# Second block's attention: probabilities as the stationary operand of the values matmul

## The chip, the cores and the metric

One core of a Trainium2 chip runs the whole program. The metric is the time of one execution on the device, in microseconds (us); the median of several runs counts. The engines are PE (matrix multiply, with PEld for its weight loads), DVE (vector), ACT (scalar), POOL and SP (which issues transfers).

## What is computed

Two transformer blocks on one sequence of 512 tokens of width 1024, in fp32. The first has a sliding-window and a differential attention and a convolutional feed-forward part. The second block, in which the change lies, has an attention over the 128 keys or so that an index picks for each query, beside a recurrent branch:

```python
logits = jnp.einsum('bthc,btkc->bthk', ql.astype(f32), c_sel)      # 16 heads
logits = logits - slopes[None, None, :, None] * dist[:, :, None, :]
logits = jnp.where(valid[:, :, None, :], logits, -jnp.inf)
p = jax.nn.softmax(logits, axis=-1)
o = jnp.einsum('bthk,btkc->bthc', p, c_sel)
...
y_attn = (o * jax.nn.silu(g_attn)) @ w_attn_proj
```

## The kernel before

Activations are held transposed: eight tiles of 128 features by 512 tokens. Every projection is a "unit" of 128 output features: 8 steps over the input features, each three matmuls with 512 moving columns (high and low parts of weights and activations, `mm3`), accumulated in a PSUM bank. Weights come in by DMA and are split into high and low parts by ACT and by DVE or POOL, some units ahead.

The order of issue isn't written out. The projection loop emits a step and then calls `sched`, which lets generators (`spawn`) go on where a small cost model (`account`) says that their engine and inputs are ready; a generator yields a hint ("T" for PE, "D" for DVE, "A" for ACT) ahead of its next operation. `account` prices each operation and keeps a clock for each engine. The prices set the order only; on the chip each engine takes its instructions in that order and waits for semaphores. All instructions go through one helper, so the trace puts nearly all of them on line 214.

The stage of the change is the loop at the end of `block2` that runs, for each of 8 pairs of heads t, the unit `q{t}` (queries) and the unit `ga{t}` (gate), and then the units `ma0` to `ma2`; behind it the loop waits until all eight results `ao` are there and goes on with the units `wa0` to `wa7`. When the queries and keys of a pair are there, a queue (one item every 2.5 us at most) starts `mla(t, b)` for the four blocks b of 128 queries, in the order 3, 2, 1, 0. Block b sees n = (b + 1) x 128 keys. One `mla`:

- logits of two heads (e = 0, 1) into two banks of the tag "lg" (two banks in all);
- on DVE, for each head, mask and distance added and the minimum taken, into `Lm`;
- on ACT, for each head, the exponential in place, with its row sums into `l`;
- on DVE the reciprocal of the two sums, and for each head `Lm` scaled by it (lines 1741 to 1744);
- for each head b + 1 transposes of 128x128 on PE into a bank of the tag "pt" (two banks), copied by ACT into `PTm`: keys on the partitions, queries along the columns;
- the values matmuls: for each key block c and head e, the values `V` (128 keys by 64) are loaded as the stationary operand and `PTm` (128 keys by 128 queries) moves through, into the 64 partitions of head e of the bank `po` (tag "o"). The output is features by queries, as the rest of the block wants it.

After the four blocks of a pair the gate `g` is multiplied with `po`, and the product is split into high and low parts `ao`. In the first block `swa` and `diff` do the same step with the probabilities loaded and the values moving; `swa` loads 64 columns of queries at a time, `diff` 128, with 128 columns of values moving.

In the names of the trace, `ps_o<-PTm,V` is a matmul that moves `PTm` over the loaded `V` into `po`, `ps_o<-vtok,PTd` is `diff`'s and `ps_o<-va,PT` is `swa`'s. An fp32 matmul shows as two records of load and matmul, one of the transposes or of the projections as one.

Of the kernel before, what the change touches and what calls it, by code (L numbers as in the profile page):

```python
# [15 lines left out]
OP = mybir.AluOpType  # L16

P = 128
S = 512
D = 1024  # L20
# [213 lines left out]
class _Build:  # L234
# [53 lines left out]
    def account(self, key, op, args, kw):  # L288
        aps = [a for a in list(args) + list(kw.values()) if isinstance(a, bass.AP)]
        outs = [a for n, a in kw.items() if n in ("out", "accum_out") and isinstance(a, bass.AP)]  # L290
        if "out" not in kw:
            outs.append(args[0])
        oid = set(id(a) for a in outs)
        n = max(a.free_size() if callable(a.free_size) else a.free_size for a in aps)
        t = self.free[key]
        t00 = t
        for a in aps:
            nm, r = self.region(a)
            f = self.wf.get(nm)
            if f and not (key == "T" and id(a) in oid):  # L300
                t = max([t] + [f.get(i, 0.0) for i in r])
            if id(a) in oid:
                f = self.rf.get(nm)
                if f:
                    t = max([t] + [f.get(i, 0.0) for i in r])
        if key == "T":
            n = outs[0].free_size() if callable(outs[0].free_size) else outs[0].free_size
            m = args[1].free_size() if callable(args[1].free_size) else args[1].free_size
            if op == "transpose":
                c = 0.109  # L310
            elif args[1].dtype == F32R:
                c = max(n / 2400.0, 0.1) + 0.003
            elif m <= 64:
                c = max(n / 930.0, 0.08)
            else:
                c = max(4 * n / 2400.0, 0.21) + 0.004
        elif key == "D":
            c = 0.07 + n * 0.00104
            if op == "tensor_copy" and not any(a.name.startswith("ps_") for a in aps):
                c = 0.07 + n * 0.00052  # L320
            if op in ("tensor_tensor_scan", "scalar_tensor_tensor"):
                c += 0.06
            elif op == "tensor_scalar" and not any(a.name.startswith("ps_") for a in aps):
                c = 0.13 + n * 0.00052
        elif key == "A":
            c = 0.094 + n * 0.000833
            if any(a.name.startswith("ps_") for a in aps):
                c -= 0.042
            c += n * 0.000182 * sum(isinstance(kw.get(x), bass.AP) for x in ("scale", "bias"))
            if "accum_out" in kw:  # L330
                c += 0.093
            if op == "activation":
                f = args[2] if len(args) > 2 else kw["func"]
                if f == AF.Tanh:
                    f = self.fam if self.fam is not None and self.fam != 3 else 0
                else:
                    f = FAM.get(f)
                if f is not None and f != self.fam:
                    self.fam = f
                    c += 1.28  # L340
        elif key == "P":
            c = 0.15 + n * 0.0021
        else:
            c = n * P * 4 / 350000.0
        e = t + c
        self.free[key] = e
        for a in aps:
            nm, r = self.region(a)
            f = (self.wf if id(a) in oid else self.rf).setdefault(nm, {})
            for i in r:  # L350
                f[i] = max(f.get(i, 0.0), e + LAT[key])
        if key != "S":
            self.fin = max(self.fin, e + LAT[key])
        self.last = (t, e)
        self.issued += 1
# [980 lines left out]
    def block2(self, nx):  # L1336
        nc, T = self.nc, self.T
        xs, rb = nx["xs"], nx["rb"]
        wuk, wuv, wrg, wrt = [], [], [], []
        for n in range(4):  # L1340
            t = self.slot("wrg")
            nc.scalar.dma_start(t, self.ins["wrg"][:, n, :])
            wrt.append(t)
        for n in range(2):
            t = self.slot("wuv")
# [341 lines left out]
        for n in range(2):  # L1687
            t = self.slot("wuk")
# [31 lines left out]
        def mla(t, b):  # L1720
            d = pair[t]
            n = (b + 1) * P
            m, l, Ls, xt = self.sm("m2", 2), self.sm("l2", 2), [], []
            yield "T"
            pls = yield from self.psw("lg", 2)
            self.logits(pls, d["q"], d["k"], b, 0, n)
            for e in range(2):
                yield "D"
                L = self.slot("Lm")
                nc.vector.tensor_tensor_reduce(out=L[:, :n], in0=Dt[b][:, :n], in1=pls[e][:, :n], op0=OP.add,  # L1730
                                               op1=OP.min, scale=SLOPES2[2 * t + e], scalar=3e38,
                                               accum_out=m[:, e:e + 1])
                self.rel(pls[e])
                Ls.append(L)
            pls = None
            for e in range(2):
                yield "A"
                nc.scalar.activation(Ls[e][:, :n], Ls[e][:, :n], AF.Exp, bias=m[:, e:e + 1], scale=-1.0,
                                     accum_out=l[:, e:e + 1])
            yield "D"  # L1740
            rr = self.sm("r2", 2)
            nc.vector.reciprocal(rr, l)
            for e in range(2):
                nc.vector.tensor_scalar(Ls[e][:, :n], Ls[e][:, :n], rr[:, e:e + 1], None, op0=OP.mult)
            for e in range(2):
                yield "T"
                pt = yield from self.psw("pt")
                for c in range(b + 1):
                    nc.tensor.transpose(pt[:, c * P:(c + 1) * P], Ls[e][:, c * P:(c + 1) * P], self.ident)
                x = self.slot("PTm")  # L1750
                yield "A"
                nc.scalar.activation(x[:, :n], pt[:, :n], AF.Copy)
                self.rel(pt)
                xt.append(x)
            Ls = None
            yield "T"
            while d["po"] is None and self.psn["o"] > 1:
                yield "T"
            if d["po"] is None:
                d["po"] = self.ps("o")  # L1760
            po = d["po"]
            for c in range(b + 1):
                for e in range(2):
                    hc = (2 * t + e) * 64
                    vt = V[c][hc // 512]
                    nc.tensor.matmul(po[64 * e:64 * e + 64, b * P:(b + 1) * P], vt[:, hc % 512:hc % 512 + 64],
                                     xt[e][:, c * P:(c + 1) * P], start=(c == 0), stop=(c == b))
            xt = None
            d["n"] += 1
            if d["n"] < 4:  # L1770
                return
            while f"ga{t}" not in T:
                yield
            yield "D"
            g = T.pop(f"ga{t}")
            nc.vector.tensor_mul(g, g, d["po"])
            self.rel(d["po"])
            self.dump(f"ao{t}", g)
            del pair[t]
            yield "A"  # L1780
            ao[t] = yield from self.split(g, None, name="ao")
# [3 lines left out]
        for t in range(8):  # L1785
            self.unit(f"q{t}", xs2, ev_q(t))
            qm["items"] += [(lambda t=t, b=b: t in pair and b in Dt and "V" in cell, mla(t, b))
                            for b in (3, 2, 1, 0)]
            self.unit(f"ga{t}", xs2, ev_act(f"ga{t}", AF.Silu))
# [154 lines left out]
```

## Time and profile before

| what | value |
|---|---|
| median of 3 runs | 1333.4 us (1333.04 to 1334.54) |
| the profiled execution's own time | 1329.96 us |
| its span, first to last instruction | 1328.1 us |
| PE busy | 1290.4 us, 97% |
| PE weight loads busy | 1065.6 us, 80% |
| DVE busy | 901.3 us, 68% |
| ACT busy | 708.0 us, 53% |
| POOL busy | 301.8 us, 23% |
| mean granted TensorE clock | 0.99 |

The durations below are from the one profiled execution, the time of the kernel from separate runs. A matmul's record lasts longer than its share of the engine, since matmuls are pipelined; what one costs is read from start to start.

### The profile page before, as it was taken

Reading aid. Unit: us, or ns where it says so; the run is one execution under the profiler, and the core shown is the slowest. Engines: PE = TensorE matmul, PEld = TensorE weight load, DVE = VectorE, ACT = ScalarE, POOL = GpSimd, SP = SyncE. Lnnn points to the kernel's source line nnn. Section 1 sums busy time; section 2 is a strip of 40 time slices with the busy share of each in tenths; the row PEclk is TensorE's granted clock in tenths of the full one; section 3 lists DMA queues with packets and bytes.
Section 4 is the critical chain, followed back from the end, with each engine's and each line's share of the span. In section 5 each row is a group of like instructions: output and inputs, shape, how many; then the busy total and the mean of one; then the engine's idle time right before and its main releaser. Section 6 shows DMA issues by size and latency. Waiting matters only on the chain.

```text
span 1328.1 us, 17863 instructions
## 1 busy us (share of the span) xinstructions
PE 1290.4 (97%) x6748; PEld 1065.6 (80%) x6748; DVE 901.3 (68%) x1586; ACT 708.0 (53%) x1258; POOL 301.8 (23%) x204
## 2 busy tenths in 40 slices
PE   9999998999999999999999988999999999999997
PEld 7788888888888888888887875888788778787886
DVE  6768768776266736674677689588989676753354
ACT  7598765344234313432344455888771778783332
POOL 4301015223034303330333353031220000010111
PEclk9999999999999999999999989999999999999998
DMA  6302240233323332333224410222223121122321
GB/s 234 89 24 64 65 146 30 64 95 96 109 81 95 95 111 80 95 95 107 85 95 132 138 48 16 64 80 79 80 94 114 64 64 48 49 63 96 95 65 64
DMA packets 34245, 113.23 MB, mean 85 GB/s; under 512 B 3824, under 2 KB 5872, under 8 KB 34160
## 3 DMA queue, kind: packets, MB, share of 16 engines
q1 hardware_dynamic: 32192, 109.48, 26.4%
q10 hardware_dynamic: 1968, 2.62, 0.6%
q8 instruction: 53, 0.87, 0.3%
q14 instruction: 32, 0.26, 0.1%
HBM read 109.99 MB, written 2.10 MB: 84 GB/s over the span
## 4 chain that ended last, share of the span: by engine, by line
PE 76%; DVE 16%; ACT 4%; issue 2%; DMA 1%; SPq 0%; POOL 0%; ACTq 0%; DVEq 0%; POOLq 0%
PE ps_mm L214 58%; PE ps_lg L214 8%; PE ps_o L214 8%; DVE c L214 3%; PE ps_pt L214 3%; DVE sq L214 1%; DVE xl L214 1%; DVE sl L214 1%; DVE score L214 1%; ACT wh L214 1%; ACT c L214 1%; DVE wl L214 1%; DVE yo L214 1%; DVE m L214 1%; ACT L214 1%
## 5 line engine op out<-in xcount | busy, mean ns | idle before, releaser
L214 PE MATMUL ps_mm<-xh,wh 128*128 128x512 f32 x840 | 336.8, 401 | 0.0
L214 PE MATMUL ps_mm<-xh,wl 128*128 128x512 f32 x840 | 331.1, 394 | 0.1
L214 PE MATMUL ps_mm<-xl,wh 128*128 128x512 f32 x840 | 330.8, 394 | 0.0
L214 POOL TENSOR_TENSOR wl<-wr,wh 128x1024 fp32r<-128x1024 f32 (+1 forms) x69 | 166.4, 2412 | 423.5 <-ACT wh L214 423.5
L214 ACT ACTIVATE wh<-wr 128x1024 fp32r<-128x1024 f32 (+1 forms) x179 | 185.4, 1038 | 130.9 <-PE ps_mm L214 96.8
L214 DVE SCALAR_TENSOR_TENSOR c<-u,vec,c 128x511 f32<-128x511 f32 (+1 forms) x128 | 171.6, 1342 | 74.8 <-ACT c L214 72.5
L214 PEld LDWEIGHTS ps_mm<-xh,wl 128*128 128x128 f32 x840 | 158.5, 189 | 38.7 <-POOL wl L214 0.8
L214 PEld LDWEIGHTS ps_mm<-xh,wh 128*128 128x128 f32 x840 | 158.7, 189 | 36.5 <-issue 2.0
L214 PEld LDWEIGHTS ps_mm<-xl,wh 128*128 128x128 f32 x840 | 158.8, 189 | 33.6 <-DVE xl L214 0.2
L214 DVE TENSOR_TENSOR wl<-wr,wh 128x1024 fp32r<-128x1024 f32 (+1 forms) x110 | 134.3, 1221 | 72.5 <-ACT wh L214 72.1
L214 ACT ACT_TABLE_LOAD x65 | 83.4, 1283 | 6.0 <-PE ps_mm L214 2.5
L214 PE MATMUL ps_mm<-acth,wh 128*128 128x512 f32 x216 | 84.3, 390 | 2.3 <-DVE fs L214 2.3
L214 PE MATMUL ps_mm<-actl,wh 128*128 128x512 f32 x216 | 84.1, 389 | 0.0
L214 PE MATMUL ps_mm<-acth,wl 128*128 128x512 f32 x216 | 84.1, 389 | 0.0
L214 ACT ACTIVATE acth<-c 128x512 fp32r<-128x512 f32 x32 | 20.2, 632 | 114.0 <-DVE c L214 111.2
L214 ACT ACTIVATE c<-c 128x512 f32<-128x512 f32 x32 | 20.2, 632 | 81.8 <-DVE c L214 81.8
L214 ACT ACTIVATE c<-u,vec 128x512 f32<-128x512 f32 x64 | 51.5, 808 | 13.5 <-DVE u L214 13.5
L214 POOL TENSOR_TENSOR sq<-sq,sq 128x256 f32<-128x256 f32 (+1 forms) x38 | 36.1, 950 | 92.4 <-ACT sq L214 77.9
L214 DVE TENSOR_TENSOR u<-ps_mm,rbn 128x512 f32<-128x512 f32 (+1 forms) x63 | 42.5, 676 | 15.1 <-PE ps_mm L214 15.1
L214 PEld LDWEIGHTS ps_mm<-acth,wh 128*128 128x128 f32 x216 | 40.5, 188 | 11.8 <-DVE fs L214 2.7
L214 POOL MEMSET skl<- 64x512 f32 x28 | 14.7, 526 | 147.4 <-PE ps_pt L214 62.7
L214 PEld LDWEIGHTS ps_mm<-actl,wh 128*128 128x128 f32 x216 | 40.5, 188 | 8.4
(407 smaller groups left out, 2640.9 us busy)
## 6 DMA issues: line engine op xcount, KB each, us to landing
wr<-in_wpk_dram SPq DMA_DIRECT2D x197, 512.0 KB, 3.6
xres<-in_xt_dram SPq DMA_DIRECT2D x8, 256.0 KB, 5.5
wr<-in_wpk_dram SPq DMA_DIRECT2D x6, 256.0 KB, 5.6
wrg<-in_wrg_dram ACTq DMA_DIRECT2D x4, 256.0 KB, 4.2
out_dram<-o SPq DMA_DIRECT2D x4, 256.0 KB, 2.2
out_dram<-o ACTq DMA_DIRECT2D x3, 256.0 KB, 2.2
con<-in_con_dram SPq DMA_DIRECT2D x1, 576.0 KB, 6.1
wuv<-in_wukv_dram ACTq DMA_DIRECT2D x2, 256.0 KB, 5.4
```

Source lines behind the costliest of these rows:

```text
L214: r = f(*a, **k)
```

## The change

In `mla` the two scalings by the reciprocal sums go; the sums of all four blocks are kept in one tile of eight columns per pair (`l8`). The values matmul has its operands exchanged: `PTm` (128 keys by 128 queries) is loaded, and the 64 columns of `V` move. The output `po` is now queries by features, 64 columns for each block and head. After the fourth block, one reciprocal of the eight sums, one product of `po` with them (broadcast over 64 columns) into `y`, four transposes of `y` on PE into a bank of the tag "pt", and the gate is multiplied with that bank. `po` is given back after the product, where before it was given back after the gate. In the cost model, the price of such a matmul falls out of a floor that is changed from 0.21 to 0.115 us; with 128 moving columns the price stays as it was.

```diff
             else:
-                c = max(4 * n / 2400.0, 0.21) + 0.004
+                c = max(4 * n / 2400.0, 0.115) + 0.004
...
-            m, l, Ls, xt = self.sm("m2", 2), self.sm("l2", 2), [], []
+            m, Ls, xt = self.sm("m2", 2), [], []
+            if "l" not in d:
+                d["l"] = self.sm("l8", 8)
...
                 nc.scalar.activation(Ls[e][:, :n], Ls[e][:, :n], AF.Exp, bias=m[:, e:e + 1], scale=-1.0,
-                                     accum_out=l[:, e:e + 1])
-            yield "D"
-            rr = self.sm("r2", 2)
-            nc.vector.reciprocal(rr, l)
-            for e in range(2):
-                nc.vector.tensor_scalar(Ls[e][:, :n], Ls[e][:, :n], rr[:, e:e + 1], None, op0=OP.mult)
+                                     accum_out=d["l"][:, 2 * b + e:2 * b + e + 1])
...
-            for c in range(b + 1):
-                for e in range(2):
-                    hc = (2 * t + e) * 64
+            for e in range(2):
+                hc = (2 * t + e) * 64
+                o = b * P + 64 * e
+                for c in range(b + 1):
                     vt = V[c][hc // 512]
-                    nc.tensor.matmul(po[64 * e:64 * e + 64, b * P:(b + 1) * P], vt[:, hc % 512:hc % 512 + 64],
-                                     xt[e][:, c * P:(c + 1) * P], start=(c == 0), stop=(c == b))
+                    nc.tensor.matmul(po[:, o:o + 64], xt[e][:, c * P:(c + 1) * P], vt[:, hc % 512:hc % 512 + 64],
+                                     start=(c == 0), stop=(c == b))
...
+            yield "D"
+            r8 = self.sm("r8", 8)
+            nc.vector.reciprocal(r8, d["l"])
+            y = self.slot("ym")
+            v3 = lambda x: x.rearrange("p (n w) -> p n w", n=8)
+            nc.vector.tensor_tensor(v3(y), v3(po), r8.unsqueeze(2).to_broadcast([P, 8, 64]), op=OP.mult)
+            self.rel(po)
+            po = None
             while f"ga{t}" not in T:
                 yield
+            yield "T"
+            pt = yield from self.psw("pt")
+            for c in range(4):
+                nc.tensor.transpose(pt[:, c * P:(c + 1) * P], y[:, c * P:(c + 1) * P], self.ident)
+            y = None
             yield "D"
             g = T.pop(f"ga{t}")
-            nc.vector.tensor_mul(g, g, d["po"])
-            self.rel(d["po"])
+            nc.vector.tensor_mul(g, g, pt)
+            self.rel(pt)
```

## Rows read from the trace of the kernel before

**Rows 1.** The page's busy time by engine: us (share of the span) xinstructions.

```profile
PE 1290.4 (97%) x6748; PEld 1065.6 (80%) x6748; DVE 901.3 (68%) x1586; ACT 708.0 (53%) x1258; POOL 301.8 (23%) x204
```

**Rows 2.** Window: length, busy of PE, PEld, DVE, ACT, POOL; clock, DMA, GB/s.

```profile
1038.00:1200.00 162.00, 162.00 (x1030) 128.88 (x1029) 109.93 (x298) 126.79 (x272) 8.63 (x13) 1.00 0.18 54
```

**Rows 3.** Waits of the weight loads, 1036 to 1215: total us, times, longest.

```profile
PEld ps_o L214 <- issue: 7.4, 22, 0.4
PEld ps_pt L214 <- issue: 2.6, 15, 0.2
...
PEld ps_o L214 <- ACT PTm L214: 1.1, 3, 0.4
...
PEld ps_o L214 <- ACT Lm L214: 0.4, 1, 0.4
```

**Rows 4.** Groups by form, 1036 to 1202: xcount | busy, mean ns | idle before.

```profile
L214 PE MATMUL ps_o<-PTm,V 128*64 128x128 f32 x320 | 23.2, 281 | 0.0
...
L214 PEld LDWEIGHTS ps_o<-PTm,V 128*64 128x64 f32 x320 | 16.9, 136 | 8.9 <-issue 7.4 <-ACT PTm L214 1.1 <-ACT Lm L214 0.4
```

**Rows 5.** Old values matmuls: chain (start, us), then timeline (start, us, engine, operation).

```profile
1088.86 1.02 PE ps_o L214 x16
...
1190.57 1.68 PE ps_o L214 x28
...
1197.60 0.40 PE L214 MATMUL ps_mm<-xh,wl 128*128 128x512 f32 x1
...
1197.92 0.44 PE L214 MATMUL ps_o<-PTm,V 128*64 128x128 f32 x4
...
1198.29 0.51 PE L214 MATMUL ps_mm<-xh,wh 128*128 128x512 f32 x1
...
1198.63 0.39 PE L214 MATMUL ps_mm<-xl,wh 128*128 128x512 f32 x1
```

**Rows 6.** Timeline of the first block's `diff`, PE, 109 to 112 us.

```profile
109.33 2.40 PE L214 MATMUL ps_o<-vtok,PTd 128*128 128x128 f32 x20
111.56 0.60 PE L214 MATMUL ps_pt<-con,Ld 128*128 128x128 f32 x4
```

**Rows 7.** Timeline of two weight loads of 128 columns behind an idle stretch.

```profile
156.65 0.30 PEld L214 LDWEIGHTS ps_o<-vtok,PTd 128*128 128x128 f32 x2 [0.37 <-ACT vtok L214]
```

**Rows 8.** Timeline of loads: `swa` (64 columns), a transpose, a sum of squares.

```profile
91.99 1.01 PEld L214 LDWEIGHTS ps_o<-va,PT 128*64 128x64 f32 x32 [0.17 <-issue]
...
809.45 0.32 PEld L214 LDWEIGHTS ps_pt<-con,kw 8*128 8x128 f32 x4 [0.36 <-issue]
...
803.06 0.55 PEld L214 LDWEIGHTS ps_pt<-ones,csq 128*64 128x64 f32 x16 [0.37 <-ACT csq L214]
803.06 0.63 PE L214 MATMUL ps_pt<-ones,csq 128*64 128x1 f32 x16
```

**Rows 9.** Timeline of PE around four transposes between projection matmuls.

```profile
1084.59 0.60 PE L214 MATMUL ps_pt<-con,Lm 128*128 128x128 f32 x4
1084.95 0.48 PE L214 MATMUL ps_mm<-xh,wh 128*128 128x512 f32 x1
1085.27 0.39 PE L214 MATMUL ps_mm<-xl,wh 128*128 128x512 f32 x1
1085.50 0.39 PE L214 MATMUL ps_mm<-xh,wl 128*128 128x512 f32 x1
```

**Rows 10.** Groups of DVE by form: xcount | busy, mean ns | idle before.

```profile
L214 DVE TENSOR_SCALAR Lm<-Lm,r 128x512 f32<-128x512 f32 x16 | 7.1, 483 | 0.3
...
L214 DVE RECIPROCAL r<-l 128x2 f32<-128x2 f32 x32 | 5.2, 163 | 12.6 <-ACT Lm L214 12.1
...
L214 DVE TENSOR_TENSOR ysw<-ps_o,r 128x512 f32<-128x512 f32 x4 | 2.8, 688 | 3.3 <-PE ps_o L214 2.6 <-issue 0.7
```

**Rows 11.** Timeline of the stage's end: last gate product, first matmul of `wa0`.

```profile
1198.43 0.69 DVE L214 TENSOR_TENSOR g<-g,ps_o 128x512 f32<-128x512 f32 x1 [0.42 <-PE ps_o L214]
...
1200.49 0.39 PE L214 MATMUL ps_mm<-aoh,wh 128*128 128x512 f32 x1
```

More of the change, by code (lines that the diff above doesn't have):

```diff
@@ L1761, in mla @@
             po = d["po"]
-            for c in range(b + 1):
-                for e in range(2):
-                    hc = (2 * t + e) * 64
+            for e in range(2):
+                hc = (2 * t + e) * 64
+                o = b * P + 64 * e
+                for c in range(b + 1):
                     vt = V[c][hc // 512]
-                    nc.tensor.matmul(po[64 * e:64 * e + 64, b * P:(b + 1) * P], vt[:, hc % 512:hc % 512 + 64],
-                                     xt[e][:, c * P:(c + 1) * P], start=(c == 0), stop=(c == b))
-            xt = None
+                    nc.tensor.matmul(po[:, o:o + 64], xt[e][:, c * P:(c + 1) * P], vt[:, hc % 512:hc % 512 + 64],
+                                     start=(c == 0), stop=(c == b))
+            xt = vt = None
             d["n"] += 1
```

## The prediction

> **What bounds the kernel now.** I read the profile's busy table first: PE is busy for 97% of the span, DVE for 68%, ACT for 53% [rows 1]. The mean hides nothing here. The stage of the change runs from the first `mla` logits at 1037 us to the first matmul of `wa0` at 1200.49 us, and the table of windows shows PE busy in all 162 of 162 us between 1038 and 1200, at a granted clock of 1.00, while DVE is busy for 110 us and ACT for 127 us [rows 2]. PE matmuls wait for no engine in that stretch; the only idle time in the list of waits is that of the weight loads around the values matmuls, mostly put down to "issue", 26 times in all (22 + 3 + 1), one for each group of values matmuls [rows 3]. So the stage costs what PE's instruction stream costs, and an edit is worth what it adds to or takes from that stream. Work taken from DVE or ACT is worth nothing as long as PE has no gap to close.
>
> **Removed from PE: the old values matmuls.** There are 160 of them (2 heads x 1, 2, 3, 4 key blocks x 8 pairs), each two records: 320 loads of 64 columns, 320 matmuls with 128 moving columns [rows 4]. The two heads write different halves of the partitions and alternate, and they run side by side: a group of 16 records lasts 1.02 us and one of 28 lasts 1.68 us, so a record costs 0.66 / 12 = 0.055 us [rows 5]. 320 x 0.055 = 17.6 us. Each group has a fixed cost besides. The group of four at 1197.92: the matmul before it started at 1197.60 and an ordinary one takes 0.23 [rows 9], so 0.09 us pass empty; 0.37 us later the next matmul starts, and that one takes 0.34 instead of 0.23, since its weights weren't loaded ahead [rows 5]. 0.09 + 0.37 + 0.11 = 0.57 us, of which 0.22 are its four records: 0.35 fixed. At 15 of the 26 ends a transpose follows [rows 3], whose load is shorter by 0.05 (0.06 against 0.11, worked out below): 0.30 there. The mean is 0.32; 26 x 0.32 = 8.3 us. Old cost: 17.6 + 8.3 = 25.9 us.
>
> **Added to PE: the new values matmuls.** Again 160 and again 320 records, but each loads 128 columns of probabilities and moves only 64 columns of values. No row has this shape, so I bound it. The moving side: 128 columns, two halves at a time, cost 0.055 a record, thus 0.11 for one alone, and 64 columns half of that, 0.055. The first block's `swa` has 64 columns loaded and 64 moving: 32 loads in 1.01 us, 16 in each half of the columns, (1.01 - 0.14) / 15 = 0.058 us a load [rows 8]. That is the lower end, 0.058 us: the load hidden. The loading side: after an idle stretch, where nothing is loaded ahead, two loads of `PTd` (128 columns, fp32) end 0.30 us after the first starts at 0.19 each, so the second starts 0.11 us after the first; the projection matmul of 1198.29, with nothing loaded ahead, is 0.11 us late as well, as above [rows 5]. Is that time from load to load or only a delay? The sums of squares answer it: loads of 64 columns with one moving column, so the matmul is next to nothing, and still 16 loads take 0.55 us, eight in each half, (0.55 - 0.14) / 7 = 0.059 us apart [rows 8]. Loads follow each other no faster than about 0.9 ns a column. For 128 columns that is 0.107 to 0.118 us. The nearest row by shape is the first block's `diff`: same stationary tile kind, 128 moving columns, 20 records from 109.33 to 111.56, 0.1115 us each [rows 6]; there load (0.11) and matmul (0.11) are equally long and one is hidden behind the other. Halving the moving columns shortens the matmul and leaves the load. I take 0.110 us a record: 320 x 0.110 = 35.2 us. The ends are 0.107 (34.2) and 0.1115 (35.7), and far below them 0.058 (18.6) if loads should overlap each other.
>
> The fixed 0.32 us a group should go: `diff`'s values matmuls, also on all 128 columns, start and end without an empty stretch (20 x 0.1115 fills 109.33 to 111.56 exactly) [rows 6].
>
> A rule against this change stands in the Trainium skill, "TensorE: Matmul & The Clock Gate", section "LDWEIGHTS (loading the stationary operand)": a load takes its number of columns divided by 1.2, in ns, whatever the rows. By it a load of 128 columns is 107 ns and one of 64 is 53 ns, and the sum would be the lower end just given, 34.2 us; the rows (0.11 and 0.058) agree.
>
> **Added to PE: transposes of y.** Four for each pair, 32 in all. Four transposes start at 1084.59; the matmul behind them is done at 1085.27, and 0.23 of that is its own, so they take 0.45 us, 0.11 each [rows 9]. 32 x 0.11 = 3.5 us.
>
> **On DVE, ACT and PSUM.** Gone are 32 reciprocals of 163 ns and 64 scalings of at most 483 ns [rows 10], some 28 us at most; added are 8 reciprocals (about 0.17 each) and 8 products of 128x512 out of PSUM like `ysw`'s, 688 ns [rows 10]: 7 us. Worth nothing, since PE's gapless stream covers it; were the cover gone, each `mla` would reach its transposes about 1 us sooner. The new products sit ahead of other DVE work for 0.7 us and hold a "pt" bank a little longer, eight times; the matmuls of the projections between run on. The planner prices a new matmul at 0.119 us (before 0.138) and a transpose at 0.109: for it PE's work is 160 x 0.138 = 22.1 before, 160 x 0.119 + 3.5 = 22.5 after. Its price moves only the order of issue, so I expect nearly the same mixture and no gain or loss from it beyond 2 us either way. At the end of the stage the last pair has a longer way: its product ran 0.14 us after the last values matmul's successor began, and PE had 1200.49 - 1198.29 = 2.2 us of `ma2` left [rows 5, 11]. Now the reciprocal, the product and the transposes must come in there: some 0.2 + 0.7 + latencies of 0.3 to 0.4 = 1.2 to 1.3 us before the transposes can run, within 2.2 us. No cost, up to 1.3 us if the last group moves to the end of `ma2`.
>
> **Sum.** 35.2 + 3.5 - 25.9 = +12.8 us on PE, all of it in a stage that PE bounds. The profiled execution has a span of 1328.1 us and took 1329.96, 1.9 us around it; that becomes 1342.8. The median of the three runs is 1333.4, 3.4 above that execution; I add the difference to the median: 1346.2 us.
>
> **The rivals.**
> 1. The load is hidden behind the 64-column matmul, 0.058 us a record: 18.6 + 3.5 - 25.9 = -3.8 us, 1329.6, faster by 0.28%. It decides at 25.9 - 3.5 = 22.4 us, that is 0.070 us a record; below that the change gains. For it: the four transposed loads of `kw` (128 columns) end 0.32 us after the first starts, 0.06 apart, so 128 columns can be loaded that fast [rows 8]. Against it: these are transposes, whose loads are 0.14 long; the loads of `PTd` and of the weights are 0.19 [rows 7, 8]. 10%.
> 2. Loads partly overlap each other, halfway between: 0.084 us, 26.9 + 3.5 - 25.9 = +4.5 us, 1337.9. For it no row; against it the 0.059 of the sums of squares. 6%. The Trainium skill, "TensorE: Matmul & The Clock Gate", section "Back-to-back issue gap", gives 81 ns a matmul at 128 moving columns for a stream of loads and matmuls, which would come out about here (an estimate, 1337); the 0.1115 of [rows 6] doesn't bear it out.
> 3. Load and matmul don't overlap at all on the same rows: 0.107 + 0.055 = 0.162 us a record, 51.8 + 3.5 - 25.9 = +29.4 us, 1362.8. Against it: `diff` would then need 0.22 us a record and has 0.1115 [rows 6]. 3%. The Trainium skill, "TensorE: Matmul & The Clock Gate", "Part 3: Packing small matmuls — row/col tiling", says that a load overlaps a matmul in flight only where the row groups differ, which is this case; the row contradicts it.
> 4. The forecast's loads, and PE waiting for the new transposes besides: in each pair some 1 us for reciprocal, product and latencies, 8 x 1 = 8 us: +20.8 us, 1354.2. For it: PE takes its work in order. Against it: the transposes are issued by a planner that waits for the product, and projections stand between. 6%.
>
> **How the numbers follow.** The forecast has 75%, with its own range 1342 to 1350 (0.107 to 0.1115 a record, 2 us of order either way, 1 us of measurement). To leave out no more than 2 in 10 the range goes to 1336.5, which takes in rival 2, and to 1352. A measurement of this kernel can tell about 0.2%, 2.7 us, from no change. Faster is rival 1 with most of its chance, 0.09; no change 0.04; slower 0.87.
>
> **What would show it.** Right: rows of `ps_o<-V,PTm` with loads of 128 columns, 64 moving, x320, and groups that last 0.11 us a record; no idle "issue" before them; the stage from first logits to `wa0` longer by about 13 us, everything after it as long as before; the scalings of `Lm` on DVE gone, DVE with some 20 us less. Wrong: groups at 0.06 us a record (rival 1), at 0.16 (rival 3), or idle time of PE before `ps_pt<-con,ym` put down to DVE (rival 4). A stage that lengthens while the groups stay short would mean that I misjudged the order of issue.

## The result and the profile after

| | before | after |
|---|---|---|
| median of 4 runs each | 1333.2 us (1330.4 to 1334.5) | 1346.0 us (1343.6 to 1347.3) |
| the profiled execution's own time | 1329.96 us | 1347.28 us |
| its span | 1328.1 us | 1345.5 us |
| stage, first `mla` logits to first matmul of `wa0` | 1037.20 to 1200.49, 163.3 us | 1041.76 to 1217.77, 176.0 us |
| from there to the end of the span | 127.65 us | 127.7 us |

The changed kernel takes 1.0098 times as long, 95% interval 1.0082 to 1.0115: 13.1 us more by the ratio, 12.8 between the medians, forecast 12.8. It lies in the stage of the change: 176.0 - 163.3 = 12.7 us. The page of the changed kernel, busy time by engine (compare [rows 1]), and the window of the stage (length, busy of PE, PEld, DVE, ACT, POOL; granted clock, DMA, GB/s; compare [rows 2]):

```profile
PE 1304.8 (97%) x6780; PEld 1088.3 (81%) x6780; DVE 884.5 (66%) x1505; ACT 709.9 (53%) x1258; POOL 302.7 (22%) x205
...
1042.00:1217.00 175.00, 175.00 (x1061) 152.46 (x1060) 89.41 (x215) 128.32 (x271) 11.04 (x14) 1.00 0.17 51
```

PE is again busy without a gap, at the same clock. DVE has 20.5 us less to do in the stage (89.4 against 109.9) and it didn't help. The groups by form, 1036 to 1220 (xcount | busy, mean ns | idle before), against [rows 4]:

```profile
L214 PE MATMUL ps_o<-V,PTm 128*128 128x64 f32 x320 | 38.2, 271 | 0.0
...
L214 PE MATMUL ps_pt<-con,ym 128*128 128x128 f32 x32 | 4.8, 272 | 0.0
...
L214 PEld LDWEIGHTS ps_o<-V,PTm 128*128 128x128 f32 x320 | 39.0, 191 | 1.9
```

As many records as before, 320, with half the moving columns; PE is busy with them for 38.2 us where it was 23.2. The loads last 191 ns each instead of 136, and they fill 39.0 us instead of 16.9: they stand close behind each other. What one costs is read from start to start (timeline of PE, then of its loads):

```profile
1098.45 0.39 PE L214 MATMUL ps_mm<-xh,wl 128*128 128x512 f32 x1
1098.69 1.89 PE L214 MATMUL ps_o<-V,PTm 128*128 128x64 f32 x16
1100.42 0.39 PE L214 MATMUL ps_pt<-con,Lm 128*128 128x128 f32 x2
```

```profile
1098.46 1.98 PEld L214 LDWEIGHTS ps_o<-V,PTm 128*128 128x128 f32 x16
1100.31 0.26 PEld L214 LDWEIGHTS ps_pt<-con,Lm 128*128 128x128 f32 x2
```

16 records take 1.73 us, 0.108 each; before, 16 took 1.02 us and 0.32 around them [rows 5]. The group starts 0.24 us after the projection matmul ahead of it, as any matmul would, so nothing is empty at its start. No wait of PE or of its loads is left in the stage, where before the loads had 26 idle stretches marked "issue" or ACT [rows 3]. To sum them, each group is counted from the end of the work before it, where an ordinary matmul would have ended by its start and its usual pace, to the start of the work after it, and to that comes what the first matmul behind the group is late beyond its own pace. Over all groups the values matmuls cost 35.0 us now (23 groups) and 25.4 before (26 groups).

One thing in the profiles must not be read as the change. Both kernels issue the same instructions up to the stage, yet it begins 4.6 us later in the execution shown of after. The windows 800 to 820 and 820 to 840, of before and then of after, show the granted clock (third figure from the end), which was lower in that execution; two windows from 807.2 to 814.0 follow, again before and then after.

```profile
800.00:820.00 20.00, 18.21 (x107) 13.22 (x106) 17.41 (x33) 14.65 (x25) 6.36 (x8) 1.00 0.00 1
820.00:840.00 20.00, 15.43 (x61) 12.05 (x60) 19.00 (x23) 10.82 (x17) 6.94 (x4) 0.91 0.21 57
```

```profile
800.00:820.00 20.00, 18.45 (x94) 12.80 (x93) 14.93 (x29) 11.76 (x21) 5.09 (x4) 0.83 0.00 1
820.00:840.00 20.00, 15.43 (x60) 12.01 (x60) 19.45 (x24) 11.86 (x19) 9.34 (x7) 0.83 0.17 48
```

```profile
807.20:814.00 6.80, 6.80 (x47) 5.27 (x47) 4.96 (x13) 6.21 (x11) 1.29 (x1) 1.00 0.00 0
...
807.20:814.00 6.80, 6.76 (x16) 3.90 (x16) 2.29 (x8) 4.62 (x8) 0.93 (x1) 0.50 0.00 0
```

In those 6.8 us PE ran at the lower of its two levels (0.50, 1.2 GHz) in after and at the upper one (1.00, 2.4 GHz) in before. Matched one by one, the same PE instructions start 1.1 us later in the execution of after at 786 us of before and 4.0 us later at 810, so this stretch holds 2.9 of the 4.6 us; another 1.1 us arose earlier, by 734 us.

The spans differ by 17.4 us, the medians by 12.8. So the experiments below are compared by the stage, which lies wholly at a clock of 1.00, and by the ratio of the timed runs. Each ratio is to runs of the kernel before from the same series; over the four series their median was 1331.6 to 1333.3 us.

### The profile page after: what moved, and what is told of

Its sections match the earlier page's. It is cut to its first block, busy times and chain, and to the rows that moved or that the text cites. A ratio compares the mean times of both kernels' runs of the same rounds, so it can differ in the third digit from the quotient of the medians.

```text
span 1345.5 us, 17850 instructions
## 1 busy us (share of the span) xinstructions
PE 1304.8 (97%) x6780; PEld 1088.3 (81%) x6780; DVE 884.5 (66%) x1505; ACT 709.9 (53%) x1258; POOL 302.7 (22%) x205
## 5 line engine op out<-in xcount | busy, mean ns | idle before, releaser
L214 ACT ACTIVATE acth<-c 128x512 fp32r<-128x512 f32 x32 | 20.2, 631 | 113.9 <-DVE c L214 111.1
L214 ACT ACTIVATE c<-c 128x512 f32<-128x512 f32 x32 | 20.2, 632 | 81.8 <-DVE c L214 81.8
L214 PEld LDWEIGHTS ps_mm<-acth,wl 128*128 128x128 f32 x216 | 40.9, 189 | 8.7
```

What stands on the lines that cost most here:

```text
L214: r = f(*a, **k)
```

## Experiments

The theory: PE's stream sets the time of the stage, and in it the load of 128 columns sets the pace of the new values matmuls, 0.11 us a record, so that halving the moving columns gained nothing. The rivals: the load is hidden and the loss is in the order of issue, in the new transposes or in the new product; or any matmul with its own load costs so much, whatever the columns. All results together, with the values matmuls summed as above:

| run | ratio to before, 95% | median us | stage us | values matmuls us |
|---|---|---|---|---|
| before | 1 | 1333.2 | 163.3 | 25.4 |
| after | 1.0098 (1.0082 to 1.0115) | 1346.0 | 176.0 | 35.0 |
| e1_halves | 1.0038 (1.0024 to 1.0052) | 1337.7 | 166.7 | 25.4 |
| e2_wide | 1.0108 (1.0084 to 1.0132) | 1347.0 | 176.5 | 35.6 |
| e3_price | 1.0116 (1.0091 to 1.0140) | 1347.9 | 176.9 | 35.0 |
| e4_no_transposes | 1.0071 (1.0046 to 1.0096) | 1342.1 | 173.2 | 35.3, 0.5 of it a wait |
| e5_before_by_pairs | 0.9960 (0.9945 to 0.9976) | 1326.9 | 157.7 | 20.2 |
| e7_before_no_scaling | 0.9995 (0.9984 to 1.0006) | 1331.9 | 163.0 | 25.2 |
| e8_half_load | 1.0041 (1.0020 to 1.0061) | 1338.4 | 167.2 | 26.0 |
| e9_fp32r | 0.9969 (0.9954 to 0.9983) | 1328.0 | 159.0 | 17.6 |
| e10_after_by_pairs | 1.0118 (1.0091 to 1.0145) | 1348.1 | 177.5 | 36.6, 1.0 of it a wait |

From `wa0` to the end every run has 127.4 to 127.7 us, so nothing of any edit is paid behind the stage.

**The moving columns, doubled.** The edit of the changed kernel:

```diff
+            elif args[1].name.startswith("PTm"):
+                c = 0.119
...
-                    nc.tensor.matmul(po[:, o:o + 64], xt[e][:, c * P:(c + 1) * P], vt[:, hc % 512:hc % 512 + 64],
+                    hd = 2 * t * 64 % 512
+                    nc.tensor.matmul(po[:, b * P:(b + 1) * P], xt[e][:, c * P:(c + 1) * P], vt[:, hd:hd + P],
```

> The changed kernel with 128 moving columns of values (both heads of the pair) instead of 64, the planner's price held at 0.119 so that the order of issue stays. The second head's matmul overwrites the first's columns, so the attention output of the first heads is wrong. Theory (load sets the pace): 128 moving columns take 0.107 to 0.11 us a record, no longer than the load, so 0.1115 instead of 0.1095 a record: +0.6 us, 1346.6, stage 176.6 us. Rival (moving columns set the pace, or load and matmul add up): 0.055 us more a record, 320 x 0.055 = +17.6 us, 1363.6.

The stage came to 176.5 us against 176.0. Twice the streaming cost 0.5 us in the stage, 0.6 in the sum of the values matmuls. A group of 16 in the timeline of PE:

```profile
1097.31 1.95 PE L214 MATMUL ps_o<-V,PTm 128*128 128x128 f32 x16
1099.09 0.38 PE L214 MATMUL ps_pt<-con,Lm 128*128 128x128 f32 x2
```

1.78 us, 0.111 a record, the figure of `diff` in the first block [rows 6]. With 64 columns or 128 the record costs nearly the same, so it isn't the moving columns that are paid for, nor the sum of load and matmul.

Single records show where the small difference comes from. Short windows part the first record of the two groups above from those behind it, first in the changed kernel and then here:

```profile
1098.69 0.22 PE L214 MATMUL ps_o<-V,PTm 128*128 128x64 f32 x1
...
1098.74 0.39 PE L214 MATMUL ps_o<-V,PTm 128*128 128x64 f32 x2
```

```profile
1097.31 0.27 PE L214 MATMUL ps_o<-V,PTm 128*128 128x128 f32 x1
...
1097.42 0.50 PE L214 MATMUL ps_o<-V,PTm 128*128 128x128 f32 x3
```

Only the step from the first record to the second follows the moving columns: 0.055 us with 64, 0.108 with 128. Every later step in either group is 0.111 or 0.112 us. So the 0.108 a record of the changed kernel is a mean of one short step and many of 0.112.

**The loaded columns, halved: side by side.** 64 columns of queries at a time, alternately into both halves of the partitions:

```diff
-                    nc.tensor.matmul(po[:, o:o + 64], xt[e][:, c * P:(c + 1) * P], vt[:, hc % 512:hc % 512 + 64],
-                                     start=(c == 0), stop=(c == b))
+                    for w in (0, 64):
+                        nc.tensor.matmul(po[w:w + 64, o:o + 64], xt[e][:, c * P + w:c * P + w + 64],
+                                         vt[:, hc % 512:hc % 512 + 64], start=(c == 0), stop=(c == b))
```

> The changed kernel, but each values matmul is split in two: 64 columns of queries are loaded at a time, alternately into the two halves of the partitions, as the first block's swa does; 640 records instead of 320, the rest as changed. Theory (the 128-column load sets the pace, 0.11 us a record): loads of 64 columns in two halves at once cost 0.029 us a record, 640 x 0.029 = 18.6 us, and each of some 23 groups gets its fixed 0.32 us back, 7.4 us; 26.0 instead of the 35.0 measured for the changed kernel's values matmuls, so 9 us less: about 1337, the stage from first mla logits to wa0 167 us instead of 176. Rival (the loss comes from the order of issue, the new product or the transposes, and the load is hidden): 1346 or, with twice the records and the fixed cost back, more.

The stage came to 166.7 us, 9.3 less than the changed kernel's, for the same mathematics with twice the instructions:

```profile
1095.98 1.15 PE L214 MATMUL ps_o<-V,PTm 128*64 128x64 f32 x32
1097.06 0.44 PE L214 MATMUL ps_pt<-con,Lm 128*128 128x128 f32 x2
```

32 records (the work of 16 before) in 1.08 us instead of 1.73. The planner's price wasn't held in this run, and it made 22 groups instead of 23; e3 and e8, below, speak against the order as the cause of the gain. The idle stretches of the loads are back with the 64 columns, as expected (waits: total us, times, longest):

```profile
PEld ps_o L214 <- issue: 7.1, 20, 0.4
PEld ps_o L214 <- ACT PTm L214: 0.7, 2, 0.4
```

**The loaded columns, halved: one half alone.** Side by side, the run above changes two things, the columns of a load and what runs beside it. This one has only the smaller load:

```diff
+            elif args[1].name.startswith("PTm"):
+                c = 0.119
...
-                    nc.tensor.matmul(po[:, o:o + 64], xt[e][:, c * P:(c + 1) * P], vt[:, hc % 512:hc % 512 + 64],
+                    nc.tensor.matmul(po[:64, o:o + 64], xt[e][:, c * P:c * P + 64], vt[:, hc % 512:hc % 512 + 64],
...
-            nc.vector.tensor_tensor(v3(y), v3(po), r8.unsqueeze(2).to_broadcast([P, 8, 64]), op=OP.mult)
+            for h in (0, 64):
+                nc.vector.tensor_tensor(v3(y[h:h + 64, :]), v3(po[:64, :]),
+                                        r8[:64, :].unsqueeze(2).to_broadcast([64, 8, 64]), op=OP.mult)
```

> The changed kernel with only the first 64 columns of queries of each block loaded, into one half of the partitions; the other 64 queries of a block get the same rows, so the attention output isn't the reference's. Still 320 records with 64 moving columns, the planner's price held at 0.119, and never two halves side by side. Theory (time follows the columns loaded, about 0.9 ns each): 0.058 us a record, 18.6 us, with 23 fixed costs of 0.32 us, 26.0 instead of 35.0: -9 us, 1337, stage 167 us. Rival (a matmul with its own load needs 0.11 us whatever its size, and the halves gained only by running side by side): 35.0 + 7.4 = 42.4 us, 1353, stage 183 us.

167.2 us, values matmuls 26.0: both as the theory had it, and 16 us from the rival.

```profile
1094.38 1.85 PE L214 MATMUL ps_o<-V,PTm 128*64 128x64 f32 x28
1096.16 0.44 PE L214 MATMUL ps_pt<-con,Lm 128*128 128x128 f32 x2
```

28 records in 1.78 us, of which some 0.15 is the empty stretch at the end: 0.058 a record, where 128 columns take 0.108 in the mean and 0.112 from step to step. Same records, same moving columns, same half of PE for all: the time follows the columns that are loaded.

**One load instead of two.** `PTm` and `V` as fp32r, which needs one record for a matmul:

```diff
-                    t = self.slot("V")
+                    t = self.slot("V", F32R)
...
-                x = self.slot("PTm")
+                x = self.slot("PTm", F32R)
```

> The changed kernel with PTm and V in fp32r, so that a values matmul is one record with one load instead of two (less precise). Theory (the loads set the pace): 160 loads of 128 columns at 0.107 to 0.11 us, 17.4 instead of 35.0 us: -17.6 us, 1328.4, stage 158.5 us, below the kernel before. Rival (the pace is set by the matmul with its few moving columns, which is no cheaper in fp32r): 0.22 us each, 1346.

159.0 us and 17.6 for the values matmuls, half of 35.0. It is faster than the kernel before, by 0.31%, at less precision in this step.

```profile
1091.77 1.64 PE L214 MATMUL ps_o<-V,PTm 128*128 128x64 f32 x14
1093.24 0.55 PE L214 MATMUL ps_pt<-con,Lm 128*128 128x128 f32 x3
```

14 records (28 in the changed kernel) in 1.47 us, 0.105 each; behind a first step of 0.028 us they follow each other at 0.112 again, as in fp32. A record costs what its load costs, in either type.

**The order of issue.** The planner told the true price:

```diff
-                c = max(4 * n / 2400.0, 0.115) + 0.004
+                c = max(4 * n / 2400.0, 0.216) + 0.004
```

> The changed kernel with the planner's price of a values matmul at 0.22 us, what the chip takes, instead of 0.119. Only the order of issue changes. Theory (PE's stream is gapless, order is worth nothing): 1346 within 2 us, stage 176 us within 1. Rival (the price below the truth misplaces the work and that is where the loss is): several us back, at or below 1341.

176.9 us; the groups were 21 instead of 23 and stood elsewhere, and the time stayed within the 1 us expected (0.3 of the 0.9 us is one wait of PE for DVE). The price that the change put in is about half of what the chip takes, and that did no harm.

**The transposes of y.**

```diff
-            yield "T"
-            pt = yield from self.psw("pt")
-            for c in range(4):
-                nc.tensor.transpose(pt[:, c * P:(c + 1) * P], y[:, c * P:(c + 1) * P], self.ident)
-            y = None
             yield "D"
             g = T.pop(f"ga{t}")
-            nc.vector.tensor_mul(g, g, pt)
-            self.rel(pt)
+            nc.vector.tensor_mul(g, g, y)
+            y = None
```

> The changed kernel without the 32 transposes of y: the gate is multiplied with y as it lies, so the attention output isn't the reference's. Theory (they cost what PE streams, 0.11 us each): -3.5 us, 1342.5, stage 172.5 us. Rival (PE waits for reciprocal and product in each pair, 1 us or more each): -3.5 - 8 = -11.5 us, 1334.5. If the transposes were hidden: 1346.

The stage is 2.8 us shorter, the ratio 0.0027 or 3.6 us lower (the intervals overlap): the price of 32 transposes, and nothing of the 8 us that PE's waiting would have given back. The stage of this run holds a wait that the changed kernel hasn't, about 0.5 us, because the last group came to stand at the very end; without it the difference is 3.3 us.

```profile
1211.13 1.10 PE L214 MATMUL ps_o<-V,PTm 128*128 128x64 f32 x8 [0.33 <-ACT PTm L214]
```

The end of the stage in the changed kernel shows how the wait was avoided (timeline, PE and DVE):

```profile
1215.58 0.56 PE L214 MATMUL ps_o<-V,PTm 128*128 128x64 f32 x4
...
1216.17 0.69 DVE L214 TENSOR_TENSOR ym<-ps_o,r 128x512 f32<-128x512 f32 x1 [1.39 <-PE ps_o L214]
...
1217.42 0.60 PE L214 MATMUL ps_pt<-con,ym 128*128 128x128 f32 x4
...
1217.77 0.48 PE L214 MATMUL ps_mm<-aoh,wh 128*128 128x512 f32 x1
```

From the last values matmuls to the transposes there are 1.84 us, the product is done at 1216.86, and PE streams `ma2` in between.

**The scalings on DVE.** The kernel before without them:

```diff
-            yield "D"
-            rr = self.sm("r2", 2)
-            nc.vector.reciprocal(rr, l)
-            for e in range(2):
-                nc.vector.tensor_scalar(Ls[e][:, :n], Ls[e][:, :n], rr[:, e:e + 1], None, op0=OP.mult)
```

> The kernel before without the 32 reciprocals and 64 scalings on DVE: the probabilities aren't divided by their sums, so the attention output isn't the reference's. Theory (PE's stream has no gap to close in this stage, DVE work is hidden): 1333 within 2 us, stage 163.3 us within 1. Rival (the vector work was part of the path): 28 us of DVE less is worth some us, 1329 or below.

163.0 us against 163.3, ratio 0.9995 with 1 in the interval. The saving that the change makes on DVE is worth nothing measurable here, even alone.

**The fixed cost of a group.** The kernel before, with the values matmuls of a pair's four blocks behind the fourth:

```diff
+            d.setdefault("xt", []).append((b, xt))
+            xt = None
+            d["n"] += 1
+            if d["n"] % 4:
+                return
             yield "T"
...
-            for c in range(b + 1):
-                for e in range(2):
...
-            d["n"] += 1
+            for b, xt in d["xt"]:
+                for c in range(b + 1):
+                    for e in range(2):
...
```

> The kernel before, with the values matmuls of all four blocks of a pair issued together behind the fourth block: the same 320 records in 8 groups instead of 26. Theory (each group of 64-column loads has a fixed cost of 0.32 us, mostly empty PE at its two ends): 18 x 0.32 = -5.8 us, 1327.4, stage 157.5 us instead of 163.3. Rival (the idle time marked issue is hidden, or is paid again as waits for the last block): 1333, no change or slower.

157.7 us, 5.6 less than before; 1326.9 us, 0.40% faster than the kernel before (interval 0.24 to 0.55%) with the same arithmetic. It beats both kernels. A group of 40, and the waits of the loads that are left in the stage:

```profile
1079.78 2.40 PE L214 MATMUL ps_o<-PTm,V 128*64 128x128 f32 x40
1082.11 0.62 PE L214 MATMUL ps_lg<-sk,sq 128*128 128x384 f32 x2
```

```profile
PEld ps_o L214 <- issue: 2.9, 8, 0.4
PEld ps_mm L214 <- issue: 0.9, 5, 0.2
PEld ps_lg L214 <- DVE m L214: 0.5, 3, 0.2
```

8 idle stretches before values matmuls instead of 26. 40 x 0.055 = 2.2 us and 0.32 fixed give 2.52 a group; the sum of the eight, 20.2, gives 2.53.

**The same grouping of the changed kernel.** If grouping helped for another reason, it should help here too:

```diff
+            d.setdefault("xt", []).append((b, xt))
+            xt = None
+            d["n"] += 1
+            if d["n"] < 4:
+                return
             yield "T"
...
-            for e in range(2):
+            for b, xt in d["xt"]:
+                for e in range(2):
...
-            d["n"] += 1
-            if d["n"] < 4:
-                return
```

> The changed kernel with the values matmuls of a pair's four blocks issued together behind the fourth, 8 groups instead of 23. Theory (groups of 128-column loads have no fixed cost at their ends; what the kernel before gained from 8 groups was the fixed cost of 64-column loads): no change, 1346 within 1.5, stage 176 us. Rival (the grouping itself helps, whatever the loads): 15 x 0.32 = -4.8 us, 1341.2, stage 171 us.

177.5 us, no gain; 40 records from 1084.96 to 1089.35 are 0.110 each, as in small groups. It is 1.5 us slower, and the end of the stage shows 1.0 of it: the last group moved to the very end of `ma2`, and there the wait of my fourth rival does appear, once; 5.36 us pass from its start to the work behind it, where the other seven groups take 4.38. Without that wait the values matmuls come to 35.7 us against 35.0: there are 15 fewer groups, and so 15 fewer of the short first steps.

```profile
1084.96 4.57 PE L214 MATMUL ps_o<-V,PTm 128*128 128x64 f32 x40
1089.35 0.48 PE L214 MATMUL ps_mm<-xh,wh 128*128 128x512 f32 x1
...
1214.73 4.57 PE L214 MATMUL ps_o<-V,PTm 128*128 128x64 f32 x40
1220.09 0.66 PE L214 MATMUL ps_pt<-con,ym 128*128 128x128 f32 x4 [0.78 <-DVE ym L214]
1220.50 0.48 PE L214 MATMUL ps_mm<-aoh,wh 128*128 128x512 f32 x1
```

## Why the prediction was right, step by step

- **What bounds the stage.** Right. PE had 162 of 162 us before [rows 2] and 175 of 175 after; the 28 us of vector work gone from the kernel before alone (e7) moved the stage by 0.3 us.
- **The old cost.** 25.9 forecast, 25.4 summed over the groups. Both halves of it stood a test in e5: 18 groups fewer saved 5.6 us of the 5.8 expected, and 0.055 us a record accounts for its groups of 40.
- **The new cost, the unknown term.** 35.2 forecast, 35.0 summed; 0.110 a record forecast, 0.108 to 0.110 measured as a mean of a group. The deciding step was to ask of the rows whether a load's 0.11 us is a delay or a pace; the sums of squares, with one moving column [rows 8], answered it, and e2 and e8 confirm it from both sides. That 0.110 met the mean so closely is partly luck: the forecast didn't see that the first step of a group is short and the others 0.112. The Trainium skill, "TensorE: Matmul & The Clock Gate", section "LDWEIGHTS (loading the stationary operand)", puts a load at its columns divided by 1.2 in ns, 107 and 53 ns for 128 and 64; the runs show steps of 0.112 and 0.058 us, a little more.
- **The transposes.** 3.5 forecast. Summed as the values matmuls are, the 32 cost 3.5 us in the changed kernel; e4 gives 2.8 by the stage, 3.3 without its wait, and 3.6 by the ratio.
- **The sum.** +12.8 forecast, +12.7 in the stage, +12.8 between the medians, 1346.2 against 1346.0. By the measured terms it is 35.0 + 3.5 - 25.4 = 13.1 us, 0.4 more than the stage grew; that rest isn't placed. A total within 0.2 us is luck, since single terms are off by up to 0.5 and the runs of one kernel differ by 4 us.
- **The rivals.** Load hidden (1329.6): against it e1, e2 and e8. Partial overlap (1337.9): 0.108 a record, not 0.084. No overlap at all (1362.8): e2's 0.111 with 128 moving columns speaks against it, since load and matmul are about 0.11 long each and would take 0.22 in turn. All records of a group lie on the same rows; the Trainium skill, "TensorE: Matmul & The Clock Gate", "Part 3: Packing small matmuls — row/col tiling", lets a load overlap matmuls in flight only where the row groups differ, and the runs don't bear that out. PE waiting for the transposes (1354.2): not in the changed kernel, once in e10.
- **What wasn't foreseen.** The planner made 23 groups of 26; for 128-column loads that changes next to nothing. Behind a group a projection matmul starts some 0.05 us late, since the load of its own weights (0.11) outlasts the last matmul of the group; a group of 12 takes 1.33 us ahead of one and 1.29 ahead of a transpose. That is within the bounds that I gave a record.

That the load sets the pace is shown: it was halved, doubled in number (fp32 against fp32r) and left alone with the moving side doubled. Why a group of 64-column matmuls costs 0.3 us at its ends isn't settled; e5 and e10 show that it belongs to groups of 64-column matmuls and is paid once a group.

## What to carry to other kernels

When operands of a small matmul are exchanged, price both sides, columns loaded and columns moved, and take the longer one. Here records whose loads fill the same columns of PE followed each other at 0.9 ns for each loaded column (0.112 us for 128, 0.058 for 64), and 64 moving columns were hardly cheaper than 128; faster came loads into the two halves in turn, one every 0.029 us (e1), and those of transposes, 128 columns every 0.06 us [rows 8]. Ask first which engine's stream has no gap in the stage; 28 us of vector work saved under a full PE were worth 0.3 us. Where a matmul uses half of the columns, put many of them behind each other: each change between such a group and full ones cost 0.3 us here, and grouping them (e5) was the only edit with the same arithmetic that beat the kernel before.

## What the runs showed of the hardware that was not expected

- fp32r with only 64 moving columns is no slower a record than fp32: 0.105 us (e9), so its one record takes half the time of the two of fp32.
- Column halves load at the same time: 0.058 us a load in one half alone (e8), and 32 records in 1.08 us, 0.15 of it at the end, when both halves alternate (e1): 0.029 each.
- The granted clock ahead of the stage differs between executions with the same instructions, 0.83 against 0.91 to 1.00 between 800 and 840 us, which holds most of the 4.6 us by which the start of the stage moved here. A difference of spans of two single profiles would have put the change at 17 us.
